# Loading the last experts' last weight tile in two column halves, with the rows that follow it split and turned in pieces of 512

## The chip, the cores and the metric

The kernel runs on one core of a Trainium2 chip. The metric is the device time of one execution in microseconds (us). Before the change three executions took 996.79 us in the median (996.57 to 997.0). Lower is better.

## What is computed

Two transformer blocks follow each other on 256 tokens of 1024 channels, in fp32. The first block ends in a mixture of 32 experts, of which each token uses two; the second block starts with a norm and a projection `w_in_2`. The end of the one and the start of the other is where the change lies:

```python
def run_block(args):
    xb, e = args
    return (jax.nn.silu(xb @ w_gate[e]) * (xb @ w_up[e])) @ w_down[e]
...
ys = lax.map(run_block, (xs, block_expert)).reshape(p_rows, d)
out = jnp.zeros((n, d), jnp.float32).at[row_token].add(ys.astype(jnp.float32) * row_gate[:, None])
...
h = rms_norm(x, norm1[l])
p = h @ w_in[l]
lru_x, lru_g, q, k, v, g, z = jnp.split(p, SPLIT_IDX, axis=-1)
```

## The kernel before

**Experts.** The 32 experts run in 8 groups of four (`for g in range(NG)`). An expert's tokens (up to 32) sit in 32 rows of the array, so the four experts of a group run beside each other. `products(g, "g")` and `products(g, "u")` (L1202) make gate and up, `turn(g)` (L1221) multiplies and transposes them, and `down(g, fs)` (L1231) multiplies by the four 128-row tiles f = 0..3 of `w_down` into two PSUM tiles of 128x512, `py0` for columns 0 to 511 and `py1` for the rest. Before the change each tile f does n = 0 and then n = 1, four experts each. `y_out(g)` (L1245) scales the rows by the gate and splits each fp32 number into a high and a low part (`yh` on ScalarE, `yl` on VectorE); in the last group it does so in four pieces of 256 columns. `combine` (L1264) multiplies the split rows back to token order (`pc`) and adds them to the residual `h`.

**The last group.** Its `w_down` is loaded by `last_loads` (L457) from the SyncE queue in 12 pieces, one per tile f and expert 28, 29, 30 (128x1024, a row of 4 KB per partition); the tiles of expert 31 come from the GpSimd queue (`last_split_loads`, L463). Ahead of the last tile PE runs `keep_warm(ps, WARM3)` (L1455), and after it `keep_warm(ps, WARM4)` (L1460): transposes with a result that nobody reads. `h_turned` (L1382) has put the transposed residual into four PSUM banks `HT[0..3]` (two of the eight channel groups k in each) ahead of time; `last_turned` (L1393) adds the turned expert rows to them, and ScalarE and VectorE copy them out, scaled, to `x32`, each engine one group of every bank. `last_rows` (L1408) then combines the rows in token order and starts the sums for the norm. The second block's first matmuls read `x32`: the unit z (L1624), then k and q (L1635), with a `w_in_2` tile that is loaded in two halves of 256 columns.

**What orders the loads.** The weights wait for free buffers in the order of the program. The load of k and q stands on ScalarE's own queue (L497, two halves of 1 MB, the k half first), those of v, lx, lg and g on SyncE's (L171). Between `last_loads` and these stands `overflow()` (L1276), a branch for experts with more tokens than their 32 rows, which is not taken with these inputs. At the end of the branch (L1278) SyncE waits for all of its loads that are still under way, and then counts up the semaphores that the branch would have counted up. The loads behind the branch, the one on ScalarE's queue too, wait for these counts.

Of the kernel before, what the change touches and what calls it, by code (L numbers as in the profile page):

```python
# [9 lines left out]
F32R = mybir.dt.float32r  # L10
# [7 lines left out]
D = 1024  # L18
# [6 lines left out]
RSTD = 5  # L25
WARM = 17
WARM3 = 3
WARM4 = 5
GAINS = 15
LEAD = 5  # L30
WARM2 = 4
# [37 lines left out]
def kernel(ctx: ExitStack, tc: tile.TileContext, *aps, dbg=None, stage=9):  # L69
    nc = tc.nc  # L70
    A = dict(zip(_INS, aps))
    out = aps[len(_INS)]
    V, S, P, G = nc.vector, nc.scalar, nc.tensor, nc.gpsimd
# [17 lines left out]
    for n in range(2):  # L91
        for a in range(2):
            ns = slice(n * 512, (n + 1) * 512)
# [99 lines left out]
    half = const.tile([128, 46], F32, name="half")  # L193
# [236 lines left out]
    def expert_src(e, m):  # L430

        return {"g": wg, "u": wu, "d": wd}[m][e].rearrange("(p k) c -> p k c", p=128)
# [20 lines left out]
            load_next2()  # L453

    last = []

    def last_loads():  # L457

        for f in range(4):
            for i, t in last:  # L460
                nc.sync.dma_start(t[:, f, :], expert_src(i, "d")[:, f, :])

    def last_split_loads():  # L463

        for f in range(4):
            t = split.tile([128, 1, D], F32, name="rawx", tag=("hi", "lo", "hi", "hi")[f], bufs=4)
            load_parts(NE - 1, "d", [(t, f, 1)], nc.gpsimd)

    def ew(e, m, k):
        return EP[e, m, k] if (e, m, k) in EP else EW[e, m][:, k, :]  # L470
# [60 lines left out]
    with ExitStack() as pp:  # L531
# [10 lines left out]
        for i in range(2):  # L542
            w = [split.tile([128, 1024], F32R, name=n, tag=n, bufs=4).rearrange("p (a b) -> p a b", a=8)
                 for n in ("hi", "lo")]
# [7 lines left out]
        for i in range(4):  # L552
            pt = psp.tile([128, 2, T], F32, name="tp", tag="tp", bufs=4)
            for kk in range(2):
                k = 2 * i + kk
                for a in range(2):
                    P.transpose(pt[:, kk, a * 128:(a + 1) * 128], h[:, a, k * 128:(k + 1) * 128], ident)
            for kk in range(2):
                k = 2 * i + kk
                S.activation(hnh[:, k, :], pt[:, kk, :], AF.Copy, scale=gm[:, k:k + 1])  # L560
            for kk in range(2):
                k = 2 * i + kk
# [7 lines left out]
        sq4, v, y = [small.tile([128, 2, 2], F32, name="sq4")] + [small.tile([128, 2], F32, name=n) for n in "vy"]  # L570
# [8 lines left out]
        t = small.tile([128, 2], F32, name="t")  # L579
# [462 lines left out]
    mx = mx_stack.enter_context(tc.tile_pool(name="mx", bufs=1, reuse_waits="tile"))  # L1042
# [14 lines left out]
    v, rs, t = [small.tile([128, 2], F32, name=n) for n in "vyt"]  # L1057
# [15 lines left out]
    def t1(n, name):  # L1073
        return mo.tile([128, 2, n], F32, name=name)
# [24 lines left out]
    fs = [t1(1, f"f{i}") for i in range(3)]  # L1099
# [25 lines left out]
    ex, d, gw = t1(4, "ex"), t1(1, "d"), t1(1, "gw")  # L1125
# [9 lines left out]
    def gates():  # L1135
        p = ps.tile([128, NE], F32, name="cnt", tag="pc", bufs=2)
        P.matmul(p, onesb, At[:, 0, :], start=True, stop=False)
        P.matmul(p, onesb, At[:, 1, :], start=False, stop=True)
        g1, g2 = t1(1, "g1"), t1(1, "g2")
        V.tensor_scalar(g1, d, 1.0, None, op0=ALU.add)  # L1140
        V.tensor_tensor(g1, g1, gw, op=ALU.mult)
        V.reciprocal(g1, g1)
        V.tensor_tensor(g2, g1, d, op=ALU.mult)
        for a in range(2):
            V.tensor_scalar(o1[:, a, :], o1[:, a, :], g1[:, a, :], None, op0=ALU.mult)
            V.scalar_tensor_tensor(gt[:, a, :], o2[:, a, :], g2[:, a, :], o1[:, a, :], op0=ALU.mult, op1=ALU.add)
        V.tensor_copy(cnti, p[0:1, :])
        V.tensor_reduce(cmax, p[0:1, :], axis=AX.X, op=ALU.max)

    with ExitStack() as pp:  # L1150
        OT, OG, CT = {}, {}, {}

        def slots_of(g):

            o = mx.tile([128, 2, 128], F32, name="oh", bufs=2)
            V.tensor_tensor(o.rearrange("p a (e c) -> p a e c", e=4),
                            rkm[:, :, 4 * g:4 * g + 4].unsqueeze(3).to_broadcast([128, 2, 4, CAP]),
                            slots[:, None, None, :CAP].to_broadcast([128, 2, 4, CAP]), op=ALU.is_equal)
            OT[g] = o
# [40 lines left out]
        P1, HT4, PY = {}, {}, {}  # L1200

        def products(g, m):  # L1202

            p = P1[m] = ps.tile([128, 512], F32, name="p1", tag="p1", bufs=2)
            for k in range(8):
                for i in range(4):
                    r = slice(32 * i, 32 * i + 32)
                    P.matmul(p[r], XS[g][:, k, r], ew(4 * g + i, m, k), start=(k == 0), stop=(k == 7))  # L1208
            if g != NG - 1:
                next_loads(g, m)  # L1210

        def next_loads(g, m):
            for i in range(4):
                if (4 * g + i, m) not in odd:
                    load_expert()

        def gate_silu():
            P1["s"] = mx.tile([128, 512], F32, name="sg")
            S.activation(P1["s"], P1["g"], AF.Silu)  # L1219
# [8 lines left out]
            HT4[g] = mx.tile([128, 4, 128], F32, name="hs")  # L1228
            S.activation(HT4[g], p, AF.Copy)  # L1229

        def down(g, fs):  # L1231
            if g not in PY:
                PY[g] = [ps.tile([128, 512], F32, name=f"py{n}") for n in range(2)]
            for f in fs:
                for n in range(2):
                    for i in range(4):
                        r = slice(32 * i, 32 * i + 32)
                        P.matmul(PY[g][n][r], HT4[g][:, f, r], ew(4 * g + i, "d", f)[:, n * 512:(n + 1) * 512],  # L1238
                                 start=(f == 0), stop=(f == 3))
            if 3 in fs:  # L1240
                next_loads(g, "d")

        ysb = {}

        def y_out(g):  # L1245

            gs = CT[g][1]
            if g < NE // 4 - 1:
                w = 512
                yh = split.tile([128, D], F32R, name="hi", tag="hi", bufs=4)  # L1250
                yl = split.tile([128, D], F32R, name="lo", tag="lo", bufs=4)
                ysb[g] = [(yh[:, c:c + w], yl[:, c:c + w]) for c in range(0, D, w)]
            else:
                w = 256
                yh = mx.tile([128, 4, w], F32R, name="yh", tag="xse")
                ysb[g] = [(yh[:, i, :], mx.tile([128, w], F32R, name="yl", tag=t, bufs=2 if t == "oh" else 1))
                          for i, t in enumerate(("sg", "hs", "oh", "oh"))]
            for i in (0, 2, 1, 3) if w < 512 else (0, 1):
                yh, yl = ysb[g][i]
                y = PY[g][i * w // 512][:, i * w % 512:i * w % 512 + w]  # L1260
                S.activation(yh, y, AF.Copy, scale=gs)
                V.scalar_tensor_tensor(yl, y, gs, yh.bitcast(F32), op0=ALU.mult, op1=ALU.subtract)

# [116 lines left out]
        HT = []  # L1380
# [12 lines left out]
        def last_turned(g):  # L1393
            c = CT[g][0].rearrange("p a t -> p (a t)")
            for q in range(2):
                for j in (q, q + 2):
                    for kk in range(2):
                        for i in range(2):
                            P.matmul(HT[j][:, kk, :], ysb[g][j][i][:, kk * 128:(kk + 1) * 128], c, start=False,
                                     stop=(kk == 1 and i == 1))  # L1400
                for k in (2 * q, 2 * q + 4, 2 * q + 1, 2 * q + 5):
                    p = HT[k // 2][:, k % 2, :]
                    if k % 2 == q:
                        S.activation(X2["x32"][:, k, :], p, AF.Copy, scale=gc[:, k:k + 1])
                    else:
                        V.tensor_scalar(X2["x32"][:, k, :], p, gc[:, k:k + 1], None, op0=ALU.mult)
# [15 lines left out]
        for g in range(NG):  # L1422
            end = g == NG - 1
            products(g, "g")
            gate_silu()
            if g == 0:
                gates()
                slots_of(1)
            else:
                for a, n, _ in HALF:  # L1430
                    combine(g - 1, a, n)
            slots_back(g)
            slots_turn(g)
            if end:
                next_loads(g, "g")
                overflow()
                last_split_loads()
                for i in range(4):
                    h_turned(i)
            products(g, "u")  # L1440
            turn(g)
            if end:
                next_loads(g, "u")
            if not end:
                gather(g + 1, 0)
                gather(g + 1, 1)
            if g < NG - 2:
                slots_of(g + 2)
            if g == 1:
                block2_consts()  # L1450
            if end:
                mr_stack.close()
                pools2()
                down(g, range(3))
                keep_warm(ps, WARM3, "p2")  # L1455
                down(g, [3])
            else:
                down(g, range(4))
            y_out(g)
        keep_warm(ps, WARM4, "p1", 2)  # L1460
        last_turned(g)
        last_rows(g)
    mx_stack.close()
# [9 lines left out]
    with ExitStack() as pc:  # L1473
# [478 lines left out]
        with ExitStack() as pp:  # L1952
# [39 lines left out]
            fs = [[small.tile([128, 1], F32, name=f"f{a}{i}") for i in range(7)] for a in range(2)]  # L1992
# [86 lines left out]
```

## Time and profile before

| | |
|---|---|
| Median of three executions | 996.79 us |
| The profiled execution | 996.26 us |
| Its span, first to last instruction | 994.2 us |
| PE busy | 869.6 us (87%) |
| Granted TensorE clock, mean | 0.922 |
| From the last tile of `w_down` to the first matmul of z | 676.2 to 684.2 us |

The profiled execution is 0.53 us below the median, and 2.06 us of it lie outside the span. A page's share of busy time says little here: the change touches some 16 us of 994, so the rows of that stretch are what is to be read. Times are counted from the span's start. "PEld" is the weight load of TensorE, "SPq" and "ACTq" are DMA issues of SyncE and ScalarE; a bracket at the end of a row says how long the engine had been idle, and what ended that.

### The profile page before, as it was taken

The numbers are of one execution on the slowest core, as the hardware profiler recorded it, in microseconds if no ns is written. First come the engines' busy times: TensorE is split into PE (matmuls) and PEld (weight loads), VectorE is DVE, ScalarE is ACT, GpSimd is POOL, SyncE is SP. The second block draws the span as 40 slices with busy tenths as digits, with TensorE's granted clock in tenths as the row PEclk, the third lists the DMA queues.
The fourth block names the chain that finished last, engine by engine and source line by source line (L and its number), as shares of the span: only waits on it lengthen the run. The fifth ranks groups of instructions, "written<-read, shape, count | busy, mean of one in ns | idle before, by whom it ended". The sixth has DMA issues, their size and how long they took to land. (4 is left out here: it accounts for less than half of the span.)

```text
span 994.2 us, 13437 instructions
## 1 busy us (share of the span) xinstructions
PE 869.6 (87%) x5577; PEld 620.3 (62%) x5578; DVE 420.4 (42%) x774; ACT 318.6 (32%) x530; POOL 101.9 (10%) x104
## 2 busy tenths in 40 slices
PE   8999999999968676786767769689989999999996
PEld 7989889786515133241422324146688799999995
DVE  6988577853011011111001110115577785555554
ACT  5665454524001100010000100004557464444444
POOL 4314020010000000000000000010000431111112
PEclk9999999999888797797879878779999999999999
DMA  9497334459999999999999999998834444556201
GB/s 299 97 389 258 119 137 169 170 179 403 427 426 429 426 426 429 428 426 428 428 424 430 428 425 429 427 408 308 336 122 154 156 156 147 201 190 212 85 2 42
DMA packets 77823, 287.82 MB, mean 289 GB/s; under 512 B 12548, under 2 KB 41407, under 8 KB 66239
## 3 DMA queue, kind: packets, MB, share of 16 engines
q1 hardware_dynamic: 74406, 281.36, 72.0%
q0 software_dynamic: 1024, 3.18, 0.8%
q10 hardware_dynamic: 2328, 2.39, 0.7%
q8 instruction: 45, 0.74, 0.3%
q14 instruction: 20, 0.16, 0.0%
HBM read 285.87 MB, written 1.05 MB: 289 GB/s over the span
## 5 line engine op out<-in xcount | busy, mean ns | idle before, releaser
L1208 PE MATMUL p<-raw,xse 128*32 128x512 f32 x1008 | 178.5, 718 | 80.7 <-DMA raw<-in_w_gate_dram 57.2
L342 PE MATMUL mm<-hnh,hi 128*128 128x256 f32 x776 | 223.9, 289 | 1.6 <-ACT cx L710 1.2
L344 PE MATMUL mm<-hnh,lo 128*128 128x256 f32 x776 | 219.9, 283 | 0.5 <-DVE lo L333 0.5
L343 PE MATMUL mm<-hnl,hi 128*128 128x256 f32 x776 | 218.6, 282 | 0.0
L333 DVE TENSOR_TENSOR lo<-raw,hi 128x1024 fp32r<-128x1024 f32 x142 | 173.2, 1224 | 83.7 <-ACT hi L332 83.6
L332 ACT ACTIVATE hi<-raw 128x1024 fp32r<-128x1024 f32 x144 | 150.8, 1057 | 97.6 <-PE po L314 37.9
L1208 PEld LDWEIGHTS p<-raw,xse 128*32 128x32 f32 x1008 | 40.0, 129 | 209.3 <-issue 93.6
L342 PEld LDWEIGHTS mm<-hnh,hi 128*128 128x128 f32 x776 | 146.6, 189 | 6.4 <-issue 2.8
L343 PEld LDWEIGHTS mm<-hnl,hi 128*128 128x128 f32 x776 | 147.5, 190 | 1.1 <-issue 0.2
L344 PEld LDWEIGHTS mm<-hnh,lo 128*128 128x128 f32 x776 | 146.1, 188 | 0.7 <-DVE lo L333 0.7
L1273 DVE TENSOR_TENSOR h<-h,pc 128x512 f32<-128x512 f32 x32 | 20.7, 683 | 140.6 <-PE pc L1271 140.6
L1191 PE MATMUL gp<-oh,xnf 128*128 128x128 f32 x256 | 64.7, 417 | 5.1 <-ACT xse L1198 5.1
L1238 PE MATMUL py<-raw,hs 128*32 128x512 f32 x480 | 66.1, 628 | 1.2 <-ACT hs L1229 0.8
L1191 PEld LDWEIGHTS gp<-oh,xnf 128*128 128x128 f32 x256 | 62.2, 334 | 6.6 <-ACT xse L1198 6.5
L1224 DVE TENSOR_TENSOR sg<-sg,p 128x512 f32<-128x512 f32 x8 | 5.5, 689 | 111.5 <-PE p L1208 111.5
L1219 ACT ACTIVATE sg<-p 128x512 f32<-128x512 f32 x8 | 4.8, 598 | 148.7 <-PE p L1208 138.4
L1229 ACT ACTIVATE hs<-p 128x512 f32<-128x512 f32 x8 | 4.8, 597 | 133.8 <-PE p L1227 133.8
L1964 POOL TENSOR_TENSOR sgf<-sgf,rsb 128x256 f32<-128x256 f32 x22 | 31.8, 1445 | 135.9 <-ACT sgf L1963 135.9
L437 POOL DMA_DIRECT2D rawx<-in_w_down_dram x4 | 2.2, 553 | 419.5 <-PE pc L1271 417.2
L1238 PEld LDWEIGHTS py<-raw,hs 128*32 128x32 f32 x480 | 21.4, 115 | 34.2 <-issue 25.4
L1196 DVE COPY xse<-gp 128x512 f32<-128x512 f32 x8 | 5.5, 692 | 74.7 <-PE gp L1191 74.7
L312 PE MATMUL po<-hi,ah 128*128 128x512 f32 x88 | 34.8, 396 | 0.0
(477 smaller groups left out, 1115.4 us busy)
## 6 DMA issues: line engine op xcount, KB each, us to landing
raw<-in_w_gate_dram SPq DMA_DIRECT2D x32, 2048.0 KB
raw<-in_w_up_dram SPq DMA_DIRECT2D x31, 2048.0 KB
raw<-in_w_down_dram SPq DMA_DIRECT2D x27, 2048.0 KB
raw<-in_w_in_dram SPq DMA_DIRECT2D x14, 2048.0 KB
raw<-in_w_ffn_in_dram SPq DMA_DIRECT2D x22, 1024.0 KB
raw<-in_w_out_dram SPq DMA_DIRECT2D x6, 2048.0 KB
raw<-in_w_ffn_out_dram SPq DMA_DIRECT2D x5, 2048.0 KB
raw<-in_w_down_dram SPq DMA_DIRECT2D x12, 512.0 KB
```

The costliest lines, as they stand in the source:

```text
L312: P.matmul(po[a, j], yh[:, ts], wh[:, 0, ns], start=(i == 0), stop=False)
L332: S.activation(hv[:, r], src[:, r], AF.Copy)
L333: lo_on[0].tensor_tensor(lv, src, hv.bitcast(F32), op=ALU.subtract)
L342: P.matmul(o, wh, xh, start=first, stop=False)
L343: P.matmul(o, wh, xl, start=False, stop=False)
L344: P.matmul(o, wl, xh, start=False, stop=last)
L1191: P.matmul(p[:, kk, :], xn[:, a, 4 * hf + kk::8], OT[g][:, a, :], start=(a == 0), stop=(a == 1))
L1196: V.tensor_copy(d, p)
L1208: P.matmul(p[r], XS[g][:, k, r], ew(4 * g + i, m, k), start=(k == 0), stop=(k == 7))
L1238: P.matmul(PY[g][n][r], HT4[g][:, f, r], ew(4 * g + i, "d", f)[:, n * 512:(n + 1) * 512], start=(f == 0), stop=(f == 3))
L1273: V.tensor_tensor(h[:, a, ns], h[:, a, ns], p, op=ALU.add)
L1964: G.tensor_tensor(t, t, rsb, op=ALU.mult)
```

## The change

In the last group, tile f = 3 of experts 28 to 30 is loaded in two halves of its columns: first the left halves of the three experts, then the right ones. `down` does f = 3 for `py0`, then `y_out` for `py0`, then `down` for `py1` and `y_out` for `py1`. The split rows come in two pieces of 512 columns and not four of 256. In `last_turned` the banks are filled in the order 0, 1, 2, 3, and each bank is copied out by one engine: 0 and 2 by ScalarE, 1 and 3 by VectorE. The bridge of warm-up transposes behind the last tile is 1 and not 5.

```diff
--- before.py
+++ after.py
@@ -25,7 +25,7 @@
 RSTD = 5
 WARM = 17
 WARM3 = 3
-WARM4 = 5
+WARM4 = 1
 GAINS = 15
 LEAD = 5
 WARM2 = 4
@@ -453,12 +453,13 @@
             load_next2()
 
     last = []
+    LAST = [(f, slice(0, D)) for f in range(3)] + [(3, slice(n * 512, (n + 1) * 512)) for n in range(2)]
 
     def last_loads():
 
-        for f in range(4):
+        for f, c in LAST:
             for i, t in last:
-                nc.sync.dma_start(t[:, f, :], expert_src(i, "d")[:, f, :])
+                nc.sync.dma_start(t[:, f, c], expert_src(i, "d")[:, f, c])
 
     def last_split_loads():
 
@@ -1228,36 +1229,37 @@
             HT4[g] = mx.tile([128, 4, 128], F32, name="hs")
             S.activation(HT4[g], p, AF.Copy)
 
-        def down(g, fs):
+        def down(g, fs, ns=range(2)):
             if g not in PY:
                 PY[g] = [ps.tile([128, 512], F32, name=f"py{n}") for n in range(2)]
             for f in fs:
-                for n in range(2):
+                for n in ns:
                     for i in range(4):
                         r = slice(32 * i, 32 * i + 32)
                         P.matmul(PY[g][n][r], HT4[g][:, f, r], ew(4 * g + i, "d", f)[:, n * 512:(n + 1) * 512],
                                  start=(f == 0), stop=(f == 3))
-            if 3 in fs:
+            if 3 in fs and 1 in ns:
                 next_loads(g, "d")
 
         ysb = {}
 
-        def y_out(g):
+        def y_out(g, half=None):
 
             gs = CT[g][1]
             if g < NE // 4 - 1:
-                w = 512
                 yh = split.tile([128, D], F32R, name="hi", tag="hi", bufs=4)
                 yl = split.tile([128, D], F32R, name="lo", tag="lo", bufs=4)
-                ysb[g] = [(yh[:, c:c + w], yl[:, c:c + w]) for c in range(0, D, w)]
+                ysb[g] = [(yh[:, c:c + 512], yl[:, c:c + 512]) for c in (0, 512)]
+                order = (0, 1)
             else:
-                w = 256
-                yh = mx.tile([128, 4, w], F32R, name="yh", tag="xse")
-                ysb[g] = [(yh[:, i, :], mx.tile([128, w], F32R, name="yl", tag=t, bufs=2 if t == "oh" else 1))
-                          for i, t in enumerate(("sg", "hs", "oh", "oh"))]
-            for i in (0, 2, 1, 3) if w < 512 else (0, 1):
+                w = 512
+                if g not in ysb:
+                    yh = mx.tile([128, 2, w], F32R, name="yh", tag="xse")
+                    ysb[g] = [(yh[:, i, :], mx.tile([128, w], F32R, name="yl", tag=t)) for i, t in enumerate(("sg", "hs"))]
+                order = (half,)
+            for i in order:
                 yh, yl = ysb[g][i]
-                y = PY[g][i * w // 512][:, i * w % 512:i * w % 512 + w]
+                y = PY[g][i]
                 S.activation(yh, y, AF.Copy, scale=gs)
                 V.scalar_tensor_tensor(yl, y, gs, yh.bitcast(F32), op0=ALU.mult, op1=ALU.subtract)
 
@@ -1393,14 +1395,14 @@
         def last_turned(g):
             c = CT[g][0].rearrange("p a t -> p (a t)")
             for q in range(2):
-                for j in (q, q + 2):
+                for j in (2 * q, 2 * q + 1):
                     for kk in range(2):
                         for i in range(2):
-                            P.matmul(HT[j][:, kk, :], ysb[g][j][i][:, kk * 128:(kk + 1) * 128], c, start=False,
+                            P.matmul(HT[j][:, kk, :], ysb[g][j // 2][i][:, (j % 2 * 2 + kk) * 128:(j % 2 * 2 + kk + 1) * 128], c, start=False,
                                      stop=(kk == 1 and i == 1))
-                for k in (2 * q, 2 * q + 4, 2 * q + 1, 2 * q + 5):
+                for k in range(4 * q, 4 * q + 4):
                     p = HT[k // 2][:, k % 2, :]
-                    if k % 2 == q:
+                    if k < 4 * q + 2:
                         S.activation(X2["x32"][:, k, :], p, AF.Copy, scale=gc[:, k:k + 1])
                     else:
                         V.tensor_scalar(X2["x32"][:, k, :], p, gc[:, k:k + 1], None, op0=ALU.mult)
@@ -1453,10 +1455,12 @@
                 pools2()
                 down(g, range(3))
                 keep_warm(ps, WARM3, "p2")
-                down(g, [3])
+                for n in range(2):
+                    down(g, [3], [n])
+                    y_out(g, n)
             else:
                 down(g, range(4))
-            y_out(g)
+                y_out(g)
         keep_warm(ps, WARM4, "p1", 2)
         last_turned(g)
         last_rows(g)
```

SyncE's queue around `last_loads`: the loads of `w_gate`, `w_up` and `w_down` for the last experts, the branch, and behind it the loads of `w_in_2`. Before:

```order
L448 DMA raw<-in_w_gate_dram 128x4096 x4
L448 DMA raw<-in_w_up_dram 128x4096 x4
L461 DMA raw<-in_w_down_dram 128x1024 x12
L1277 TENSOR_LOAD cmax
L1277 ISA x2
L1278 COMPARE_AND_BRANCH
L1278 UNCONDITIONAL_BRANCH
L171 DMA raw<-in_w_in_dram 128x8x512 x4
```

Now:

```order
L448 DMA raw<-in_w_gate_dram 128x4096 x4
L448 DMA raw<-in_w_up_dram 128x4096 x4
L462 DMA raw<-in_w_down_dram 128x1024 x9
L462 DMA raw<-in_w_down_dram 128x512 x6
L1279 TENSOR_LOAD cmax
L1279 ISA x2
L1280 COMPARE_AND_BRANCH
L1280 UNCONDITIONAL_BRANCH
L171 DMA raw<-in_w_in_dram 128x8x512 x4
```

Nine loads of 512 KB stay, three become six of 256 KB, and the loads behind the branch keep their place.

ScalarE's queue from the transposed products (`hs`) to the copies of the turned rows (`x`, from the banks `ht`); the DMA rows are the two halves of k and q, and the brackets name the semaphores that a row waits for (DMAHW0 to 7 count SyncE's and ScalarE's loads). Before:

```order
L1229 ACTIVATE hs<-p_4472 128x512 [waits PE_49,Activation_49]
L497 DMA raw<-in_w_in_dram 128x8x256 [waits DMAHW4_49,DMAHW2_49]
L497 DMA raw<-in_w_in_dram 128x8x256 [waits DMAHW4_49]
L1261 ACTIVATE yh<-py_4516,gs 128x256 [waits DVE_49,PE_49,Activation_49]
L1261 ACTIVATE yh<-py_4517,gs 128x256 [waits PE_49]
L1261 ACTIVATE yh<-py_4516,gs 128x256 [waits DVE_49]
L1261 ACTIVATE yh<-py_4517,gs 128x256 [waits DVE_49]
L1404 ACTIVATE x_4500<-ht,gc 128x256 [waits PE_49] x2
L1404 ACTIVATE x_4500<-ht,gc 128x256 [waits DVE_49] x2
```

Now:

```order
L1230 ACTIVATE hs<-p_4475 128x512 [waits PE_49,Activation_49]
L498 DMA raw<-in_w_in_dram 128x8x256 [waits DMAHW5_49,DMAHW4_49]
L498 DMA raw<-in_w_in_dram 128x8x256 [waits DMAHW7_49]
L1263 ACTIVATE yh<-py_4519,gs 128x512 [waits DVE_49,PE_49,Activation_49]
L1263 ACTIVATE yh<-py_4520,gs 128x512 [waits PE_49]
L1406 ACTIVATE x_4503<-ht,gc 128x256 [waits DMAHW2_49,PE_49]
L1406 ACTIVATE x_4503<-ht,gc 128x256
L1406 ACTIVATE x_4503<-ht,gc 128x256 [waits PE_49]
L1406 ACTIVATE x_4503<-ht,gc 128x256
```

The two DMA issues stand ahead of the first split in both; behind them are two splits of 512 columns where four of 256 stood.

PE from tile f = 3 to the first turned rows (`py` is the down product, `raw` and `rawx` the tiles of experts 28 to 30 and 31, `ht` a bank of turned rows). Before:

```order
L1238 MATMUL py_4516<-raw,hs 32x512 [waits DMAHW7_49]
L1238 MATMUL py_4516<-raw,hs 32x512 [waits DMAHW0_49]
L1238 MATMUL py_4516<-raw,hs 32x512 [waits DMAHW1_49]
L1238 MATMUL py_4516<-rawx,hs 32x512 [waits DMASW0_49]
L1238 MATMUL py_4517<-raw,hs 32x512 x3
L1238 MATMUL py_4517<-rawx,hs 32x512
L300 MATMUL warm<-ident,ones 128x128 x5
L1399 MATMUL ht<-ct,yh 128x256 [waits Activation_49]
L1399 MATMUL ht<-ct,yl 128x256 [waits DVE_49]
L1399 MATMUL ht<-ct,yh 128x256
```

Now:

```order
L1239 MATMUL py_4519<-raw,hs 32x512 [waits DMAHW7_49]
L1239 MATMUL py_4519<-raw,hs 32x512 [waits DMAHW0_49]
L1239 MATMUL py_4519<-raw,hs 32x512 [waits DMAHW1_49]
L1239 MATMUL py_4519<-rawx,hs 32x512 [waits DMASW0_49]
L1239 MATMUL py_4520<-raw,hs 32x512 [waits DMAHW2_49]
L1239 MATMUL py_4520<-raw,hs 32x512 [waits DMAHW3_49]
L1239 MATMUL py_4520<-raw,hs 32x512 [waits DMAHW4_49]
L1239 MATMUL py_4520<-rawx,hs 32x512
L300 MATMUL warm<-ident,ones 128x128
L1401 MATMUL ht<-ct,yh 128x256 [waits Activation_49]
L1401 MATMUL ht<-ct,yl 128x256 [waits DVE_49]
```

The three right halves have waits of their own now, one warm-up transpose is left of five, and the first eight products of turned rows wait for one split piece.

## Rows read from the trace of the kernel before

**Rows 1.** The chain of waits, 655 to 705 us: start, us, what.

```profile
677.29 0.41 ACTq L497
...
677.75 15.03 DMA raw<-in_w_in_dram
...
692.82 3.72 PE mm L1635 x16
```

**Rows 2.** PE in order of time at 692 us: start, us, what, idle before.

```profile
692.82 3.72 PE L1635 MATMUL mm<-x,raw 128*128 128x256 f32 x16 [0.48 <-DMA raw<-in_w_in_dram]
```

**Rows 3.** Weight loads of the down products, 669 to 678 us, and what ended each wait.

```profile
673.47 0.11 PEld L1238 LDWEIGHTS py<-raw,hs 128*32 128x32 f32 x1 [1.02 <-DMA raw<-in_w_down_dram]
...
677.20 0.11 PEld L1238 LDWEIGHTS py<-raw,hs 128*32 128x32 f32 x1 [0.88 <-SPq L1278]
```

**Rows 4.** DMA issues of SyncE in order of time, 640 to 700 us.

```profile
642.83 24.24 SPq L461 DMA_DIRECT2D raw<-in_w_down_dram  x12
677.72 17.11 SPq L171 DMA_DIRECT2D raw<-in_w_in_dram  x4
```

**Rows 5.** The same view from 560 us on: four issues back to back.

```profile
622.43 1.75 SPq L448 DMA_DIRECT2D raw<-in_w_up_dram  x4
```

**Rows 6.** Stretches: busy us and count of each engine, then PEclk, DMA share, GB/s.

```profile
664.00:672.00 8.00, 7.09 (x38) 2.26 (x38) 2.92 (x12) 0.60 (x1) 0.00 (x0) 0.79 1.03 410
...
674.00:676.00 2.00, 2.00 (x18) 0.85 (x10) 0.00 (x0) 0.00 (x0) 0.00 (x0) 1.00 0.40 156
...
681.00:692.00 11.00, 11.00 (x76) 9.44 (x74) 10.16 (x23) 7.20 (x18) 0.53 (x1) 1.00 1.06 376
...
697.00:700.50 3.50, 3.50 (x18) 3.06 (x17) 0.00 (x0) 0.00 (x0) 0.00 (x0) 1.00 1.05 385
```

**Rows 7.** ScalarE in order of time, 677 to 681 us.

```profile
677.29 1.04 ACTq L497 DMA_DIRECT2D raw<-in_w_in_dram  x2
678.46 0.47 ACT L1261 ACTIVATE yh<-py,gs 128x256 fp32r<-128x256 f32 x1 [12.88 <-PE py L1238]
```

**Rows 8.** Instructions on `py`: duration ns min/median/max, first and last start.

```profile
L1261 ACT ACTIVATE hi<-py,gs x14: 687/687/689, 272.8 to 622.6; 128x512 fp32r<-128x512 f32 x14
L1262 DVE SCALAR_TENSOR_TENSOR lo<-py,gs,hi x14: 750/751/752, 273.6 to 623.3; 128x512 fp32r<-128x512 f32 x14
L1261 ACT ACTIVATE yh<-py,gs x4: 467/474/476, 678.5 to 680.2; 128x256 fp32r<-128x256 f32 x4
L1262 DVE SCALAR_TENSOR_TENSOR yl<-py,gs,yh x4: 476/484/485, 679.0 to 680.7; 128x256 fp32r<-128x256 f32 x4
```

**Rows 9.** PE in order of time, 676 to 685 us.

```profile
676.17 1.65 PE L1238 MATMUL py<-raw,hs 128*32 128x512 f32 x5
...
678.52 0.59 PE L1238 MATMUL py<-rawx,hs 128*32 128x512 f32 x1
679.04 1.38 PE L300 MATMUL warm<-ident,ones 128*128 128x128 f32 x10
680.18 0.36 PE L1399 MATMUL ht<-ct,yh 128*128 128x256 f32 x1
...
682.17 0.28 PE L1271 MATMUL pc<-yh,ct 128*128 128x256 f32 x1
...
684.16 1.07 PE L1624 MATMUL mm<-x,wz 128*32 128x256 f32 x16
```

**Rows 10.** The chain of waits at 976 us: a product of 128x512 on its path.

```profile
976.59 0.24 PE po L314
```

**Rows 11.** Other stretches, columns as in rows 6.

```profile
640.00:655.00 15.00, 12.37 (x69) 8.35 (x62) 3.07 (x6) 0.98 (x2) 2.72 (x5) 0.79 1.00 417
...
663.00:665.60 2.60, 0.97 (x8) 0.56 (x4) 1.95 (x5) 0.60 (x1) 0.00 (x0) 1.00 1.04 414
665.60:667.26 1.66, 1.63 (x9) 0.37 (x12) 1.30 (x7) 0.00 (x0) 0.00 (x0) 0.55 1.01 402
667.26:669.60 2.34, 2.34 (x16) 0.70 (x8) 0.28 (x2) 0.00 (x0) 0.00 (x0) 0.59 1.04 415
```

## Prediction

> **What bounds the kernel now.** I read the chain of waits first, since 16 us of 994 are touched and the page's shares are averages over all of it. Around the change the chain does not run through the expert rows at all. It runs through a load: ScalarE issues the two halves of the k and q columns of `w_in_2` at 677.29, the second half lands 15 us later, and PE goes on at 692.82 [rows 1]. PE's own timeline says the same from the other side: it had finished everything in front of these products, and sat idle 0.48 us for that load [rows 2]. So the work between the last tile of `w_down` and the k products has 0.48 us of slack, and whatever is saved in it beyond nothing goes into this wait.
>
> What starts the load? The order of ScalarE's queue shows it behind the branch's end, which waits for every load that SyncE has under way. PE's last wait for a tile of `w_down` ends at 677.20, put down to that very branch line [rows 3], and ScalarE issues 0.09 us later. So the landing of the last piece of tile f = 3 (call it T, 677.20) starts the load that sets the end. The change works on what comes after T, and touches T itself only by the shape of the loads.
>
> **The change, part by part.**
>
> *The halves of the load.* Removed: three loads of 512 KB with rows of 4 KB. Added: six of 256 KB with rows of 2 KB. The bytes stay. From the end of the wait for expert 30's tile f = 2 (673.47) to the same for f = 3 (677.20) lie 3.73 us for three loads [rows 3], 1.24 us each. Stretches filled with rows of 4 KB move 410 GB/s, one filled with the 2 KB rows of `w_in_2` 385 [rows 6]. If the pieces slow in this ratio, 3.73 us become 3.73 x 410/385 = 3.97, and T moves by +0.24. The lower bound is 0 (the rate falls to 156 GB/s at 674 to 676 because some DMA engines have run dry, and those that carry the rest may not feel the row length); the upper one takes the slowest stretch with short rows, 376 GB/s: +0.34 [rows 6]. I take +0.25, since the 385 come from rows of just this length.
> The three extra issues on SyncE cost some 0.44 us each (1.75 us for four [rows 5]). Twelve were issued by 642.83 + 24.24 = 667.07 [rows 4]; three more end long before T and are free. The next thing on SyncE is the branch, which waits for T anyway. ScalarE and the v load queue behind it as before, so both move with T.
>
> The Trainium skill's page "DMA: Bandwidth & Descriptors", section "Anatomy of one DMA", speaks against this edit: it puts a fixed price of about 2.0 us beside the bytes of each DMA. Three more loads would by it be +6.0 us, an estimate from that page, if nothing hid it. The trace does not agree for loads in a row: 512 KB at 410 GB/s are 1.28 us, and they land 1.24 us apart, which leaves no room for a fixed price.
>
> *Products of tile f = 3.* PE does `py0` for all four experts as soon as the left halves are in, so after T only experts 30 and 31 of `py1` are left. Before, T was followed by 1.9 us of products (677.20 to 678.52 + 0.59) [rows 3, 9]. `py0` is now done before T; `py1` ends at about T + 1.0, some 0.9 us earlier.
>
> *What is queued behind.* Here the gain gets stuck. The split of `py0` is a ScalarE instruction, and it stands in the queue behind the two DMA issues, which wait for T and take 1.04 us; the first split now starts at 678.46, 0.13 us after they end [rows 7]. That is T + 1.26, and it stays T + 1.26: with `py0` ready before T, ScalarE's queue is late next, not PE. With T at 677.45 the first split starts at 678.71.
>
> *Splits.* Four of 256 columns (474 ns on ScalarE, 484 on VectorE) become two of 512 (687 and 750 ns) [rows 8]. ScalarE: 678.71 to 679.40 and to 680.09. VectorE follows: 679.43 to 680.18, then to 680.96. The four before ended at 681.2 (last start 680.7 [rows 8]).
>
> *Bridge and turned rows.* Five warm-up transposes ran to about 680.2, where the turned rows began [rows 9]; one ends near 679. It covers nothing that the turned rows wait for: their second product needs the low part at 680.18. Of sixteen products at 0.12 us apart (680.18 to 682.17 [rows 9]) the first runs early, seven run from 680.23 to 681.07, eight to 682.03; the second low part (680.96) is there in time. That is 0.14 us earlier than 682.17. Each bank copied out by one engine removes the waits of one engine for the other; the copies stay 4 and 4 and end before PE needs them.
>
> *Rows in token order.* Sixteen products of 256 columns, 0.12 us each, become eight of 512 at 0.24 [rows 10]: 1.92 us either way. The z unit then starts at 684.02 and not 684.16 [rows 9].
>
> **The sum.** PE reaches the second k and q half at 692.82 - 0.48 - 0.14 = 692.20, and that half lands at 692.8 + 0.25 = 693.05. PE waits some 0.8 us in place of 0.48, and everything behind moves by +0.25. Nothing later takes part in the change. Against the profiled execution: 996.26 + 0.25 = 996.5. That execution lies 0.53 us under the median, so the median goes from 996.79 to **997.0**. 0.2% of the time, about what a measurement of this kernel can tell from no change, is 2.0 us.
>
> **Rivals.**
>
> *The load stops binding.* With another mix of loads in flight after T, the second half could land before PE wants it. Then PE's own 692.20 counts: -0.62, 996.2. For: the half took 15 us for 1 MB because other loads ran beside it, 376 GB/s in all [rows 6], so its landing hangs on their sharing. Against: the same loads follow in the same order, all released by T. 0.09.
>
> *The clock falls, and the kernel is slower.* The bridge loses four transposes, while PE now idles from about 679 to 680.2 (but for one product), and from the end of `py0` to T before that. The trace shows what can follow: at 663.0 to 665.6 PE was busy 0.97 of 2.6 us, and the granted clock then read 0.55 and 0.59, so the lower level, 1.2 GHz, for most of 4 us [rows 11]. From 680.2 to 692 PE is busy throughout, so a low stretch counts in full, less 0.8 us that the load hides. The stretch of rows 11 (about 0.9 of 1.66 and 0.82 of 2.34 us, 3.4 us in all) costs half of that, 1.7: +0.25 + 1.7 - 0.8 = +1.1, 997.9. At 640 to 655 the mean was 0.79, so some 6.3 us at 1.2 GHz [rows 11]; such a one costs 3.15: +0.25 + 3.15 - 0.8 = +2.6, **999.4**, slower. It decides from about 5.1 us at the lower level on. Against: one transpose and the first product of turned rows still stand in the gap. Short 0.13, long 0.06.
>
> *Each extra load has a price after all.* If the three additional loads delay T by an issue each, T moves by 0.25 + 3 x 0.44 = +1.6, 998.4. The spacing in rows 3 speaks against it: 0.04.
>
> **How the numbers follow.** My forecast, that the load binds and T moves by 0 to 0.35, has 0.65 (its own range 996.7 to 997.3). The rivals have 0.09, 0.13, 0.06 and 0.04, and 0.03 stays for what the rows don't show (0.02 faster, 0.01 slower). Within 2.0 us lie the forecast, the freed load, the short fall and the priced loads: 0.91. Slower: 0.06 + 0.01. Faster: 0.02. The range goes from the freed load, 996.2, to the short fall of the clock, 997.9, plus 0.2 for the spread of the runs shown: 996.2 to 998.1. It leaves out the long fall, the priced loads and the rest, 0.13.
>
> **What would show it.** In the new profile the chain should still go through ScalarE's issue of k and q and their landing, with PE waiting 0.6 to 1.0 us for it. The last wait of the down products should end at 677.2 to 677.6, the first split start 1.2 to 1.3 us after that although `py0` is done before, and the turned rows end near 682.0. The forecast is wrong if that wait for the load is gone, if the granted clock drops below full between 679 and 692, or if T moves by more than 0.5 us.

## The result, and the profile after

The change makes the kernel slower by half a per cent. The prediction said 997.0 us, within 0.2% of before.

| | before | after |
|---|---|---|
| Median, six executions each | 996.08 us | 1000.85 us (1000.06 to 1002.74) |
| Ratio, 95% interval | | 1.0051 (1.0041 to 1.0061) |
| The profiled execution | 996.26 us | 1000.94 us |
| Its span | 994.2 us | 998.8 us |
| Granted TensorE clock, mean | 0.922 | 0.924 |
| First matmul of z | 684.16 us | 684.14 us |
| Second half of k and q reached by PE | 692.82 us | 696.76 us |

The chain of waits after runs through the same places as [rows 1]:

```profile
677.62 0.41 ACTq L498
...
678.07 18.64 DMA raw<-in_w_in_dram
696.76 3.72 PE mm L1639 x16
```

ScalarE's issue moved by 0.33 us, but the load behind it takes 18.64 us and not 15.03. PE in order of time shows who pays (compare [rows 2, 9]):

```profile
677.25 0.85 PE L1239 MATMUL py<-raw,hs 128*32 128x512 f32 x3
...
678.47 0.49 PE L300 MATMUL warm<-ident,ones 128*128 128x128 f32 x2
679.52 0.38 PE L1401 MATMUL ht<-ct,yh 128*128 128x256 f32 x1 [0.57 <-ACT yh L1263]
680.31 0.39 PE L1401 MATMUL ht<-ct,yl 128*128 128x256 f32 x1 [0.40 <-DVE yl L1264]
...
682.20 0.40 PE L1273 MATMUL pc<-yh,ct 128*128 128x512 f32 x1
...
684.14 1.07 PE L1628 MATMUL mm<-x,wz 128*32 128x256 f32 x16
687.07 7.17 PE L1639 MATMUL mm<-x,raw 128*128 128x256 f32 x32 [1.86 <-DMA raw<-in_w_in_dram]
696.76 3.72 PE L1639 MATMUL mm<-x,raw 128*128 128x256 f32 x16 [2.52 <-DMA raw<-in_w_in_dram]
```

The weight loads of the last `py1` (compare [rows 3]):

```profile
677.25 0.33 PEld L1239 LDWEIGHTS py<-raw,hs 128*32 128x32 f32 x3 [0.31 <-issue]
```

At the z unit PE is where it was, to 0.02 us. Then PE waits twice, 1.86 us for the first half of k and q, for which it had not waited before, and 2.52 us for the second. Less the 0.48 us that it had waited before, these are 3.90 of the 3.94 us between 692.82 and 696.76.

ScalarE and SyncE in order of time (compare [rows 4, 7]):

```profile
677.62 1.04 ACTq L498 DMA_DIRECT2D raw<-in_w_in_dram  x2
678.78 1.27 ACT L1263 ACTIVATE yh<-py,gs 128x512 fp32r<-128x512 f32 x2 [13.60 <-PE py L1239]
```

```profile
677.82 17.00 SPq L171 DMA_DIRECT2D raw<-in_w_in_dram  x4
```

The first SPq issue is v. Before, it came at 677.72 with k/q at 677.29: k/q had a **head start** of 0.43 us. After, it comes 0.20 us behind k/q.

What the two queues moved in equal stretches of 6 us, beginning 0.71 us after the k/q issue (q10 is ScalarE's queue, q1 SyncE's; columns: packets, MB, share of 16 engines). Before, 678.00 to 684.00 and then 684.00 to 690.00:

```profile
q10 hardware_dynamic: 1125, 1.14, 60.4%
q1 hardware_dynamic: 318, 0.65, 30.5%
...
q1 hardware_dynamic: 757, 1.52, 68.9%
q10 hardware_dynamic: 752, 0.77, 37.7%
```

After, 678.33 to 684.33 and 684.33 to 690.33:

```profile
q10 hardware_dynamic: 823, 0.84, 48.1%
q1 hardware_dynamic: 475, 0.97, 43.2%
...
q1 hardware_dynamic: 750, 1.50, 68.5%
q10 hardware_dynamic: 754, 0.76, 38.1%
```

In the second stretch the queues move the same number of packets, 754 and 750. A packet of k/q is 1 KB and one of v 2 KB, so k/q gets a third of the bytes. In the first stretch k/q moved 302 packets fewer than before, because v joined it earlier. The fourth microsecond behind the k/q issue shows it, before (680.29 to 681.29) and after (680.62 to 681.62):

```profile
q10 hardware_dynamic: 370, 0.38, 108.0%
q1 hardware_dynamic: 2, 0.00, 1.1%
```

```profile
q1 hardware_dynamic: 124, 0.25, 68.1%
q10 hardware_dynamic: 138, 0.14, 39.7%
```

Before, k/q still had the engines all but to itself; after, v was already beside it. At the later pace of 754 in 6 us the 302 packets take 2.4 us. The other 1.2 us of the 3.6 lie at the end. Behind 692 a third queue (q0, GpSimd's) joins. k/q's last packets, 693.33 to 696.33 us after the change:

```profile
q1 hardware_dynamic: 289, 0.59, 52.6%
q0 software_dynamic: 116, 0.41, 35.8%
q10 hardware_dynamic: 171, 0.16, 15.8%
```

171 packets in 3 us are under half of the earlier pace. The Trainium skill, page "DMA: Bandwidth & Descriptors", section "Queues, rings and completion order", says that each DMA engine serves in turn the queues that have work for it, several descriptors at a time. The equal counts agree with the turns; how many descriptors a turn has they don't tell.

From here on the delay is passed on, and a little is added. The four products `rsp` (duration ns min/median/max, first and last start), before the change:

```profile
L293 PE MATMUL rsp<-dg,ones x4: 379/379/483, 700.7 to 809.8; 128*128 128x256 f32 x4
```

and after:

```profile
L293 PE MATMUL rsp<-dg,ones x4: 379/379/483, 704.6 to 814.6; 128*128 128x256 f32 x4
```

+3.9 at the first and +4.8 at the last. Between them lies a stretch at the lower clock (columns as in [rows 6]) that the trace of before does not have:

```profile
740.30:744.00 3.70, 3.70 (x16) 3.34 (x15) 0.92 (x3) 1.62 (x3) 0.00 (x0) 0.54 0.00 0
```

### The profile page after: what moved, and what is told of

Same layout as the page of the kernel before. It is cut to its first block, busy times and chain, and to the rows that moved or that the text cites. A ratio compares the mean times of both kernels' runs of the same rounds, so it can differ in the third digit from the quotient of the medians.

```text
span 998.8 us, 13405 instructions
## 1 busy us (share of the span) xinstructions
PE 869.4 (87%) x5561; PEld 616.1 (62%) x5562; DVE 419.9 (42%) x772; ACT 317.9 (32%) x528; POOL 101.6 (10%) x104
## 5 line engine op out<-in xcount | busy, mean ns | idle before, releaser
L1239 PE MATMUL py<-raw,hs 128*32 128x512 f32 x480 | 64.0, 614 | 1.8 <-DMA raw<-in_w_down_dram 1.1
L1239 PEld LDWEIGHTS py<-raw,hs 128*32 128x32 f32 x480 | 17.4, 113 | 37.3 <-issue 28.8
```

## The experiments

**The theories.** Each line that begins with "Measured" gives a median, its ratio to the kernel before in the same round, and the 95% interval of the ratio. T is the landing of the last piece of `w_down`, as in the prediction.

*Theory 1, the head start.* SyncE's loads and ScalarE's take the eight semaphores DMAHW0 to 7 in turn. At the branch's end SyncE counts these up in order, each as soon as its last load has landed (not all of them after the last landing, as the section on the kernel before says), and only then goes on to v. The k/q issue waits for one of them: DMAHW2 before, DMAHW5 after (the brackets in ScalarE's queue, above), since three more loads came ahead. The counts stand in the traces some 0.07 us apart: before, that of DMAHW2 at 677.25 with five more behind it, up to 677.60; after, that of DMAHW5 at 677.52 with two more, up to 677.65. So fewer counts lie between the release of k/q and that of v, and v shares the engines earlier. *Theory 2:* the halved pieces with rows of 2 KB, just ahead of T, slow the load. *Theory 3:* each further load costs. A falling clock is a rival of the prediction.

| kernel | loads more than before | k/q issued | v issued | head start | chain: load |
|---|---|---|---|---|---|
| after_pad5 | 8 | 686.36 | 687.19 | 0.83 | 14.38 us |
| before | 0 | 677.29 | 677.72 | 0.43 | 15.03 us |
| after_merge3 | 0 | 677.61 | 678.04 | 0.43 | 15.07 us |
| full_loads | 0 | 677.08 | 677.52 | 0.44 | 15.07 us |
| before_cols1 | 1 | 677.23 | 677.58 | 0.35 | 17.13 us |
| before_cols2 | 2 | 676.61 | 676.90 | 0.29 | 18.22 us |
| after | 3 | 677.62 | 677.82 | 0.20 | 18.64 us |
| before_cols3 | 3 | 677.19 | 677.39 | 0.20 | 18.75 us |
| before_pad3 | 3 | 684.77 | 684.98 | 0.21 | 18.75 us |
| after_warm5 | 3 | 677.24 | 677.45 | 0.21 | 18.91 us |
| before_cols5 | 5 | 677.40 | 677.47 | 0.07 | 19.08 us |

The times of issue are from the ACTq and SPq rows of each kernel in order of time, and the load is its row in the chain of waits, as shown above.

### More loads ahead, in halves of the partitions

```diff
-                nc.sync.dma_start(t[:, f, :], expert_src(i, "d")[:, f, :])
+                for p in ((slice(0, 64), slice(64, 128)) if 3 * f + i - NE + 4 < 3 else (slice(0, 128),)):
+                    nc.sync.dma_start(t[p, f, :], expert_src(i, "d")[p, f, :])
```

(`< 3` for before_pad3, 6 and 7 for the others; after_pad5 has the same in the changed kernel with 5.)

before_pad3. 

> The kernel before, with tile f = 0 of experts 28 to 30 loaded in two halves of its partitions: three more loads some 10 us ahead of T (the landing of the last w_down piece), the rest as before. Nothing else of the change is in it. Theory 1, the head start: three more loads move every later load on by three of the eight load semaphores, so that the k/q issue is released when three fewer of SyncE's eight counts at the branch end are left; the v load then follows the k/q load after 0.20 us and not 0.43, takes part of the rate, and the second k/q half lands at 696 to 697 as in the changed kernel; time 999.5 to 1001. Theory 2, the shape: what delays the k/q half are the short rows and pieces just ahead of T; then it lands at 692.8 and the time is 996 to 996.5.

Measured 1006.19 us, 1.0101 (1.0085 to 1.0116).

after_pad5. 

> The changed kernel, with five more loads some 8 to 10 us ahead of T (f = 0 of the three experts and f = 1 of two in halves of their partitions): eight more than before the change, so that the semaphores come round to the same place. Theory 1, the head start: k/q is issued 0.43 us ahead of v again, its second half lands at about 693.1, time 996.0 to 996.7. Theory 2, the shape of the halved pieces: still 696.7 and 1000.9. Theory 3, each further load costs: later than the changed kernel, 1001 to 1003.

Measured 1003.96 us, 1.0075 (1.0061 to 1.0088).

before_pad6. 

> The kernel before, with six more loads ahead (f = 0 and f = 1 of the three experts in halves of partitions). Theory 1: the last piece of w_down then sits on the last of the eight semaphores, and k/q waits for the first of them, which is counted up as soon as the eighth last load has landed; so k/q is issued some 7 us ahead of T, beside the last pieces of w_down, lands before PE needs it, and holds T back by up to 1.8 us: 995.5 to 997.5, and no wait of PE for k/q. Theory 2: as before, k/q issued just behind T, landing at 692.8, 996 to 996.5.

Measured 1006.32 us, 1.0107 (1.0091 to 1.0122).

before_pad7. 

> The kernel before, with seven more loads ahead. Theory 1: the last piece sits on the first of the eight semaphores, so seven counts follow it; k/q is issued after the first of these, v after the seventh, a head start of 0.5 us and not 0.43: the second half lands at 690 to 692.5, PE does not wait for it or by under 0.3 us, 995.4 to 996.1. Theory 2: as before, 692.8, 996 to 996.5.

Measured 1004.94 us, 1.0092 (1.0077 to 1.0107).

All four times missed every expectation, for a reason of the edit: T itself came 7 to 10 us late (with pieces cut by columns, below, it does not). While pieces of 64 partitions were loaded, the rate was under three quarters of that with whole ones; the stretch in before_pad3:

```profile
655.00:670.00 15.00, 12.18 (x94) 5.36 (x92) 2.67 (x7) 0.60 (x1) 0.00 (x0) 0.99 1.03 297
```

and in the kernel before:

```profile
655.00:663.00 8.00, 8.00 (x73) 3.00 (x71) 0.00 (x0) 0.00 (x0) 0.00 (x0) 0.97 1.03 408
```

So the total times say nothing on the theories. What counts from the issue on does (table): before_pad3, without the halved last tile, takes 18.75 us, and after_pad5, with it, 14.38. before_pad6 has k/q ahead of T, as Theory 1 said. ScalarE and PE there:

```profile
678.37 1.59 ACTq L498 DMA_DIRECT2D raw<-in_w_in_dram  x2
```

```profile
694.11 1.07 PE L1625 MATMUL mm<-x,wz 128*32 128x256 f32 x16
695.11 10.63 PE L1636 MATMUL mm<-x,raw 128*128 128x256 f32 x48
```

Its v is issued at 687.58, so k/q comes 9.2 us ahead of the branch's end, and PE runs through z and all of k and q without a wait. before_pad7 has none either, with a head start of 0.93 us. This head start, and the 0.83 us of after_pad5, missed their expectations too (0.5 and 0.43): the order of the counts is as expected, but 0.38 us pass between the last two counts of after_pad5 (686.66 to 687.04), and 0.39 us behind the last of before_pad7 (685.69 to 686.08), in place of 0.07. Why stays open. after_pad5 waits for the same semaphore as the kernel before, so its shorter load goes with the longer head start and not with the semaphore.

### The same without moving T

```diff
-        for f in range(4):
-            for i, t in last:
-                nc.sync.dma_start(t[:, f, :], expert_src(i, "d")[:, f, :])
+        for f in range(4):
+            for n in ((slice(0, 512), slice(512, D)) if f == 0 else (slice(0, D),)):
+                for i, t in last:
+                    nc.sync.dma_start(t[:, f, n], expert_src(i, "d")[:, f, n])
```

before_cols3. 

> The kernel before, with tile f = 0 of experts 28 to 30 loaded in two halves of its columns (all 128 partitions, so at nearly the full rate): three more loads again, but the last tile is loaded whole, as before the change. Theory 1, the head start: k/q is issued 0.20 us ahead of v, its second half takes 18.5 to 18.8 us from the issue and not 15.0, PE waits some 2.5 us for it, time 999.5 to 1001. Theory 2, the halved pieces just ahead of T: nothing changes, 15.0 us and 996 to 996.5.

Measured 1002.29 us, 1.0062 (1.0048 to 1.0075). Chain, and PE's stretches from 692 us (columns as in [rows 6]):

```profile
677.65 18.75 DMA raw<-in_w_in_dram
...
696.44 5.41 PE mm L1636 x16
```

```profile
692.00:696.00 4.00, 1.92 (x9) 1.34 (x8) 2.04 (x12) 2.10 (x2) 0.00 (x0) 1.00 1.05 388
696.00:700.00 4.00, 3.56 (x9) 2.84 (x10) 0.00 (x0) 0.09 (x1) 0.00 (x0) 0.61 1.05 386
```

The whole loss, with nothing of the change but its count of loads, and none of it ahead of T: k/q was issued at 677.19, 0.10 us earlier than before. It came out above the expected range; in the profiled execution (1002.5 us) the clock did that: PE was busy 1.92 of 4 us while it waited, then had 0.61 granted, so the lower level for most of that stretch, and 3.72 us of products took 5.41.

```diff
-    LAST = [(f, slice(0, D)) for f in range(3)] + [(3, slice(n * 512, (n + 1) * 512)) for n in range(2)]
+    LAST = [(slice(0, 2), slice(0, D)), (2, slice(0, D))] + [(3, slice(n * 512, (n + 1) * 512)) for n in range(2)]
```

after_merge3. 

> The changed kernel, with f = 0 and f = 1 of each expert loaded in one piece of 1 MB: three loads fewer, so as many as before the change, while the last tile still comes in halves. Theory 1: k/q is issued 0.43 us ahead of v again and its second half lands 15 us later, at about 693; PE waits under 1 us for it; time 996.0 to 997.0, which is what the prediction on record said of the change. Theory 2, the halved pieces: 18.6 us and 1000.9 as in the changed kernel.

Measured 996.3 us, 1.0004 (0.9995 to 1.0013). Chain:

```profile
678.06 15.07 DMA raw<-in_w_in_dram
...
693.17 3.72 PE mm L1639 x16
```

All of the change is in it, halves included, and the loss is gone: Theory 2 falls. Theory 3 falls by after_pad5, which has eight loads more than before and the shortest k/q load of the table, and by the k/q issue of before_cols3, which three more loads did not make later.

### How the head start acts

The edit is that of before_pad3, with halves of the columns, for one, two and five pieces.

before_cols1. 

> The kernel before, with f = 0 of one expert loaded in two halves of its columns: one more load, so the semaphores are moved on by one and k/q should be issued some 0.36 us ahead of v (between 0.43 and 0.20). Theory 1a, the size of the head start sets how much of k/q goes alone: from issue to landing 15.0 + 3.6 x (0.43 - 0.36) / 0.23 = 16.1 us, time 997 to 998. Theory 1b, a step: what counts is whether the first k/q issue, 0.41 us long, is over when v's begins; then 18.6 to 18.8 us as at 0.20, time 999.5 to 1001.

Measured 999.65 us, 1.0023 (1.0012 to 1.0034).

before_cols2. 

> The same with two more loads; head start some 0.29 us. Theory 1a (size): 15.0 + 3.6 x (0.43 - 0.29) / 0.23 = 17.2 us, time 998 to 999. Theory 1b (step): 18.6 to 18.8 us, 999.5 to 1001.

Measured 1001.37 us, 1.0054 (1.0035 to 1.0073).

before_cols5. 

> The same with five more loads; head start some 0.07 us. Theory 1a (size): 15.0 + 3.6 x (0.43 - 0.07) / 0.23 = 20.6 us, time 1002 to 1003.5. Theory 1b (step): 18.6 to 19 us, 999.5 to 1001.

Measured 1001.62 us, 1.0048 (1.0032 to 1.0064).

Each load more takes 0.07 us from the head start. The landing follows neither a line (1a) nor one step (1b): +2.1 us at 0.35, +3.2 at 0.29, +3.6 at 0.20, +4.1 at 0.07. Most is lost within the first 0.14 us. The time of before_cols1 lies in the range of 1b although its load does not; in its profiled execution the products behind the wait took 5.41 us, as in before_cols3. The packets show where the steepness comes from. Up to the 16th packet of v, 3.7 us pass from its issue at a head start of 0.43, 3.3 at 0.35, 3.1 at 0.29, 2.7 at 0.20 and 2.8 at 0.07. So 0.23 us less head start bring v's data 1.2 us nearer to the k/q issue (4.15 us behind it before, 2.94 after). Until then 819 packets of k/q have started before the change, and 637, 503, 347 and 295 in before_cols1, before_cols2, the changed kernel and before_cols5. Why v's data come later behind a longer head start stays open; the first k/q issue lasts 0.41 us, so a v issue at 0.35 is the first that begins before that one is over.

```diff
+            elif nm == "v":
+                t = R2[nm] = raw_tile([128, 8, 512])
+                for c in (0, 256):
+                    nc.sync.dma_start(t[:, :, c:c + 256], wcols("w_in_2", c0 + c, 256))
```

after_v_rows. 

> The changed kernel, with v loaded in two halves of 256 columns, so that its rows in memory are as short as those of k/q (1 KB in place of 2 KB); the head start of k/q stays at 0.20 us. Theory 1, the two queues take turns row by row, so that k/q gets a third of the rate beside rows twice as long: it now gets half, its second half lands at 689 to 691 and not 696.7, PE does not wait for it: 995.5 to 996.8. A rival (the head start itself sets the landing, not the lengths of the rows): 18.6 us and 1000.9 still.

Measured 994.9 us, 0.9986 (0.9977 to 0.9995). Head start still 0.21 us (677.80 and 678.01). The queues, 681 to 684 us, and PE:

```profile
q10 hardware_dynamic: 530, 0.54, 54.4%
q1 hardware_dynamic: 526, 0.54, 53.2%
```

```profile
685.90 10.63 PE L1643 MATMUL mm<-x,raw 128*128 128x256 f32 x48 [0.52 <-DMA raw<-in_w_in_dram]
```

With rows as short as its own k/q gets half of the bytes. PE waits 0.52 us for the first half and not at all for the second. So turns by equal numbers of rows are shown as the mechanism (how many rows a turn has is not): at the same head start the load binds or not by the length of the neighbour's rows.

### The rest of the change

after_warm5 (`WARM4 = 5`). 

> The changed kernel, with the bridge of 5 transposes as before the change (WARM4 = 5). Theory 1: nothing, 18.6 us from issue to landing and 1000.9. The rival of the prediction on record, a clock that falls for want of the bridge: 996.5 to 998.

Measured 1001.38 us, 1.0056 (1.0042 to 1.0069): the bridge has no part in the loss.

full_loads (`LAST` of four whole tiles f). 

> The changed kernel without its halved loads: 12 whole pieces as before, and the rest of the change (py0 ahead of py1, two splits of 512 columns, banks each to one engine, bridge of 1). Theory 1: k/q is issued 0.43 us ahead of v and lands at 692.8, PE waits 0.5 to 0.8 us for it, 996 to 996.5: the loss of the change sits in its loads alone. If the rest of the change has a part in the loss: over 997.

Measured 997.17 us, 1.0012 (1.0003 to 1.0021). That is over 997, so by the expectation the rest of the change has a part in the loss, of 0.1%. Its profiled execution, 996.04 us, shows the k/q load at 15.07 us and the second half reached at 692.65, so nothing lost in this place; where the other executions have their 0.1% stays open. The larger part of the half per cent is not in this part (1.0051 against 1.0012); after_merge3, which has this rest of the change too, shows 1.0004.

### k and q on SyncE's queue

```diff
-                    nc.scalar.dma_start(t[:, :, c:c + 256], wcols("w_in_2", c0 + c, 256))
+                    nc.sync.dma_start(t[:, :, c:c + 256], wcols("w_in_2", c0 + c, 256))
```

after_kq_sync. 

> The changed kernel, with the two halves of k and q issued by SyncE ahead of v instead of by ScalarE: one queue, so k/q has no other large load beside it, whatever the semaphores do. Theory 1, the sharing of the two queues: both halves land by 688, PE waits for none of them; the splits no longer stand behind the issues, so the turned rows end about 1 us earlier: 994 to 995.5, faster than both. Theory 2 (what the halved pieces leave behind slows the load): PE still waits for the second half, over 998.

Measured 994.3 us, 0.9986 (0.9977 to 0.9995). ScalarE and PE:

```profile
676.89 0.69 ACT L1263 ACTIVATE yh<-py,gs 128x512 fp32r<-128x512 f32 x1 [11.34 <-PE py L1239]
677.88 0.69 ACT L1263 ACTIVATE yh<-py,gs 128x512 fp32r<-128x512 f32 x1 [0.30 <-PE py L1239]
```

```profile
682.29 1.07 PE L1628 MATMUL mm<-x,wz 128*32 128x256 f32 x16
683.29 10.63 PE L1639 MATMUL mm<-x,raw 128*128 128x256 f32 x48
694.62 3.62 PE L1639 MATMUL mm<-x,raw 128*128 128x256 f32 x16
```

No wait for k/q is left, the first split begins at 676.89, ahead of the k/q issue (677.10), and z starts 1.85 us earlier than in the changed kernel. Of these, 0.74 us are no gain of the edit that was shown: T itself came earlier in this execution (the row of `py1` that begins at 677.25 in the changed kernel begins at 676.51). This is faster than the changed kernel, and by little than the kernel before.

before_kq_sync. 

> The kernel before, with the two halves of k and q issued by SyncE ahead of v. Theory 1: the 0.48 us that PE waits for the second half are gone, and the first split starts some 0.3 us earlier: 995.0 to 995.8. A rival: v now starts 1 us later and becomes what PE waits for, then 996 to 997.

Measured 995.13 us, 0.9993 (0.9984 to 1.0002): in the range, but not told apart from no change.

full_loads_kq_sync. 

> As full_loads, with k and q issued by SyncE ahead of v. What it says is what the halved loads are worth once k/q does not bind: with T 0.25 us earlier but py0 only ready after T, the turned rows should end some 0.5 to 0.9 us later than in the changed kernel with the same queue (which took 994.3): 994.8 to 995.2. If the halved loads are worth nothing, 994.0 to 994.5.

Measured 994.69 us, 0.9991 (0.9982 to 1.0): z at 683.06, so the halved loads bring 0.77 us in this pair of traces, which issue k/q within 0.04 us of each other. The total lies between the two expectations, and its ratio and that of after_kq_sync have overlapping intervals: no gain of the halved loads is shown in the time.

## Why the prediction was wrong

- *"T moves by +0.24"*, taken as +0.25: it came out so in this pair of traces, but is not shown. In the new trace the last weight load of `py1` from the halved pieces starts about 677.47 (the row's end less one duration), 0.27 us later than 677.20 [rows 3]. after_warm5, with the same loads, issues k/q 0.38 us earlier than the changed kernel, so traces differ by more than this term.
- *`py0` before T, `py1` ends at about T + 1.0*: right; the bridge behind it begins at 678.47.
- *The first split stays at T + 1.26, behind the two issues*: right. Forecast 678.71, measured 678.78; the issues end at 678.66. after_kq_sync shows the cause: without them it starts at 676.89.
- *Splits, turned rows, combine, z at 684.02*: right to 0.12 us (684.14); of the gain of 0.14 us that it adds up, 0.02 came.
- *The clock stays*: 1.00 from 679 to 696.7 in the new trace. The lower level came later, at 740.3, in a part of the program where 0.9 us was added.
- *No price for each load*: right; in before_cols3 three more loads leave the k/q issue where it was, and in after_pad5 eight more leave the load itself no longer. The section "Anatomy of one DMA" of the Trainium skill's page "DMA: Bandwidth & Descriptors", which the prediction names here, has its 2.0 us for loads that GpSimd issues. These are SyncE's, and the sum uses nothing of it.
- **The step that failed is the last of the sum:** "that half lands at 692.8 + 0.25 = 693.05". It was taken that what starts 0.25 us later lands 0.25 us later. It landed 3.7 us later still: 18.64 us after its issue and not 15.03. Its ground stands with the first rival: "the same loads follow in the same order, all released by T". They do follow in the same order, but on two queues, and what sets the sharing is the time between the two releases, which fell from 0.43 to 0.20 us. Both were within reach of the prediction: the two issue times in [rows 1, 4], and the semaphores in the two listings of ScalarE's queue, DMAHW2 and DMAHW5.
- The first rival saw that the landing "hangs on their sharing", but gave it a gain alone. Its mirror, a landing some microseconds later, had no chance and no price, though the row of 15.03 us for 2 MB told that the load had little over a third of the 376 GB/s of [rows 6].

The rest was sound: the load bound, as in the forecast with 0.65, but the term for its landing was +0.25 and measured +3.94. None of the three signs came that the prediction names for being wrong: the wait was there, the clock stayed full between 679 and 692, and T moved by less than 0.5 us. What gave it away was the wait itself, 1.86 + 2.52 us where it says 0.6 to 1.0.

## What to carry to other kernels

When the path runs through a transfer, ask what shares the engines with it and which of the two is released first, to a tenth of a microsecond; a change in the number of loads elsewhere can turn that. A load that the path needs belongs on the same queue ahead of its rivals, or beside rivals with rows no longer than its own; in the changed kernel each of these took the loss back and left 0.14% less time than the kernel before takes; in the kernel before, the first can't be told from no change. Cut loads by columns and not by partitions, and look at an engine's own queue of issues when a result that is ready early isn't taken up.

## What the runs showed that was not expected

- Two queues side by side moved equal numbers of packets: 754 of 1 KB against 750 of 2 KB, and 530 against 526 where both were 1 KB. The queue with short rows gets fewer bytes.
- 0.14 us less head start cost 3.2 us of landing, 0.36 us cost 4.1.
- A program's count of loads can be felt by later ones, through the turn of eight semaphores: one load more moved the issue of v by 0.07 us against that of k/q.
- Pieces of 64 partitions with rows of 4 KB: 297 GB/s in their stretch, against 408.
- A wait of PE is sometimes followed by a stretch at the lower clock: 0.61 granted in 696 to 700 us of before_cols3, after 2.5 us of waiting, which made the products behind it 1.7 us longer. Of the seven traces in which PE waits over 2 us in all for k/q, four show it (before_cols1, 3 and 5, after_warm5); the changed kernel does not.
